# The first turn of a narrow expert: its float32 weight chunk becomes a split one

## The chip, the cores and the metric

The kernel runs on one core of one Trainium2 chip. The metric is the device time of one execution in microseconds (us); lower is better. Three executions of the kernel before took 1529.44, 1529.49 and 1529.63 us, so the median is 1529.49 us.

## What is computed

The reference is a two-layer hybrid encoder on 256 tokens of width 1024. What concerns this change is its last block, a top-2-of-8 expert SwiGLU:

```python
def swiglu(xn, w_gu, w_down):
    g, u = jnp.split(xn @ w_gu, 2, axis=-1)
    return (jax.nn.silu(g) * u) @ w_down

def moe_swiglu(xn, router, w_gu, w_down):
    ...
    for e in range(N_EXPERTS):
        out = out + comb[..., e:e + 1] * swiglu(xn, w_gu[e], w_down[e])
    return out
```

All weights are float32. Each expert has 1024 x 7168 gate and up weights and 3584 x 1024 down weights.

## The kernel before

**Positions, turns, chunks.** The eight experts are processed one after another, in an order that is found at run time; a place in this order is a position (`expert(e, ...)` with e from 0 to 7). Positions 1, 3, 5 and 7 and position 0 are wide (128 token slots); positions 2, 4 and 6 are narrow (64 slots). The hidden width 3584 is worked through in 7 turns (j = 0 to 6) of 512 columns. A turn takes four weight chunks of 128 x 2048 float32 (1 MB each) for gate and up: g0 and g1 for the gate product `pg`, u0 and u1 for the up product `pu`. From the second turn on it also takes two chunks d0 and d1 for the down products of the turn before. Turn 0 has none of these, as nothing is there to multiply yet.

**Split chunks.** `chunk()` takes a landed chunk and splits it in two halves of 1024 columns. For each half ScalarE (ACT) makes a rounded copy hi (line 168, a CAST) and VectorE (DVE) makes the rest lo = raw - hi (line 169, a TENSOR_TENSOR). Tiles for hi and for lo come from rings of NPART = 4 halves each, so that at most two chunks are split ahead of the matmuls that read them. The matmuls (PE) then work on hi and on lo in the faster of the two number formats, `float32r`.

**Narrow positions.** The activations of a narrow position have their hi and lo parts side by side in the 128 columns of the stationary operand, so a split chunk takes four matmuls with hi and four with lo (`narrow`, line 1124). One chunk of each turn, u1, is not split at all: `whole_chunk()` hands out the landed tile, and four float32 matmuls read it directly (line 1193; in the trace each of them is two weight loads and two matmul records). So a narrow turn before has one float32 chunk and three split ones for gate and up, and two split ones for the down products if j is above 0.

**Around turn 0.** The tail of the position before is still under way when the first turn of a narrow position begins: two scalings of its output on DVE (`yl`, line 1235), four scatter products on PE (`so`, lines 1242 and 1243) and four additions to the accumulator on DVE (`accum`, line 1245). Within the turn, `fold` brings the two halves of `pg` together (two copies on ACT, lines 1146 and 1147, one addition on DVE, line 1148), and `gate` makes the hidden values `eh` (an activation on ACT, line 1204, and a product on DVE, line 1206). At the start of the next turn `eh` is transposed on PE (line 1155) and split on ACT and DVE (lines 1054 and 1055).

**Order.** The order of the instructions on each engine is made by a planner from the order of the program, its dependencies and a timing model; `tc.issue_after` adds an edge. `casts` is the list of all hi casts so far: `casts[-1]` is the last one that was written in the program before this point. The DMAs that fetch the chunks are issued by SyncE (SP) in the order of the program, 13 chunks ahead, into a ring of raw tiles; a DMA can start when the last reader of the tile's earlier content is done.

Of the kernel before, what the change touches and what calls it, by code (L numbers as in the profile page):

```python
# [81 lines left out]
def _build(ctx, tc, io, cap):  # L82
# [17 lines left out]
    def f32(ap):  # L100
        return ap.bitcast(F32)
# [4 lines left out]
    def acc_tile(name="acc"):  # L106
        return psA.tile([P, 512], F32, tag="acc", name=name)
# [44 lines left out]
    def split(raw, n=CH, pieces=2, apart=()):  # L152

        cut = (n // 2 + P - 1) // P * P
        parts = []
        for a, b in ((0, cut), (cut, n)):
            if len(parts) in apart:  # L160
                both = rawp.tile([P, CH], F32R, tag="raw", name="apart")
                hi, lo = both[:, :CH // 2], both[:, CH // 2:]
            else:
                hi = hip.tile([P, CH // 2], F32R, tag="hi", name="hi")
                lo = lop.tile([P, CH // 2], F32R, tag="lo", name="lo")
            step = (b - a) * 2 // pieces
            for i in range(0, b - a, step):
                done[:] = (S.copy(hi[:, i:i + step], raw[:, a + i:a + i + step]),  # L168
                           V.tensor_sub(lo[:, i:i + step], raw[:, a + i:a + i + step],  # L169
                                        f32(hi[:, i:i + step])))  # L170
                casts.append(done[0])
            parts.append((hi, lo))

        def at(a, b):
            hi, lo = parts[a >= cut]
            o = cut if a >= cut else 0
            return hi[:, a - o:b - o], lo[:, a - o:b - o]
        return at
# [761 lines left out]
    def fetch():  # L940
        n, (ap, pieces) = next(source)
        ahead.append(load(ap, pieces=pieces, spare=kinds[n] == "s"))
        kinds.append(kinds[-(NRAW + 6)])
# [167 lines left out]
    def whole_chunk():  # L1111
        if not ahead:
            fetch()
        return ahead.popleft()

    def chunk(pieces=2):
        return split(whole_chunk(), pieces=pieces)

    def narrow(ps, xs, ws, first, last):

        n = len(xs)
        for part in range(2):
            for i, (x, w) in enumerate(zip(xs, ws)):
                ins = PE.matmul(ps, x, w[part], start=first and i == part == 0,  # L1124
                                stop=last and part == 1 and i == n - 1)
        return ins

    def expert(e, g, following):
# [4 lines left out]
        def gate_up(j, gu):  # L1133
            pz = acc_tile("gu")
            for kh in range(2):
                w = chunk()
                ws = [w(kk * 512, (kk + 1) * 512) for kk in range(4)]
                moving(pz, [(xg[:, k * P:(k + 1) * P], xg[:, D + k * P:D + (k + 1) * P])
                            for k in range(kh * 4, kh * 4 + 4)],
                       ws, kh == 0, kh == 1)  # L1140
            return pz

        def fold(pg):

            sg = work.tile([P, 512], F32, tag="w2", name="esg", bufs=w2b)
            S.copy(sg[:HALF], pg[HALF:])
            S.copy(sg[HALF:], pg[:HALF])
            V.tensor_add(sg, sg, pg)
            return sg

        def turn_narrow(j, h):

            pt = tr_tile("ht")
            for i in range(4):
                ins = PE.matmul(pt[:, i * HALF:(i + 1) * HALF], h[:, i * P:(i + 1) * P], both,  # L1155
                                start=True, stop=True)
            return pt, ins

        def rows_narrow(j, pt):
            o = (j % 2) * D  # L1160
            side_by_side(ht[:, o:o + 512], pt[:, :4 * HALF])

        def step_narrow(j, h):

            xs = [xg[:, k * P:(k + 1) * P] for k in range(KD)]
            tiles = [(f * 512, (f + 1) * 512) for f in range(4)]  # L1170

            def parts(w):
                return [w(*sl) for sl in tiles]
            pg, pu = acc_tile("gu"), acc_tile("gu")
            g0 = chunk()
            g1 = chunk()
            last = narrow(pg, xs[:4], parts(g0), True, False)
            u0 = chunk()
            if j:
                with tc.issue_after(last.ins):  # L1180
                    pt, last = turn_narrow(j - 1, h)
                with tc.issue_after(casts[-1].ins):
                    rows_narrow(j - 1, pt)
            with tc.issue_after(last.ins):
                narrow(pg, xs[4:], parts(g1), False, True)
            u1 = whole_chunk()
            d0 = chunk() if j else None
            narrow(pu, xs[:4], parts(u0), True, False)
            d1 = chunk() if j else None
            with tc.issue_after(casts[-2 if j else -1].ins):  # L1190
                sg = fold(pg)
            for kk in range(4):
                last = PE.matmul(pu, f32(xs[4 + kk]), u1[:, kk * 512:(kk + 1) * 512],  # L1193
                                 start=False, stop=kk == 3)
            with tc.issue_after(casts[-1].ins):
                h = gate(sg, pu)
            if j:
                down(j - 1, 0, d0)
                down(j - 1, 1, d1)
            return h  # L1200

        def gate(pg, pu):
            sg = pg if two else work.tile([P, 512], F32, tag="w2", name="esg", bufs=w2b)
            S.activation(sg, pg, AF.Silu, scale=g.cw[:, 1:2])
            h = work.tile([P, 512], F32, tag="w2", name="eh", bufs=w2b)
            V.scalar_tensor_tensor(h, pu, g.cw[:, 1:2], sg, op0=ALU.mult, op1=ALU.mult)
            return h
# [11 lines left out]
        def down(j, n, w=None):  # L1219
            if w is None:  # L1220
                w = chunk(4 if e == NE - 1 and j == 6 else 2)
            o = (j % 2) * D
            if two:
                return narrow(py[n], [ht[:, o + f * P:o + (f + 1) * P] for f in range(4)],
                              [w(f * 512, (f + 1) * 512) for f in range(4)], j == 0, j == 6)
            return moving(py[n],
                   [(ht[:, o + f * P:o + (f + 1) * P], ht[:, o + 512 + f * P:o + 512 + (f + 1) * P])
                    for f in range(4)],
                   [w(f * 512, (f + 1) * 512) for f in range(4)], j == 0, j == 6)
# [18 lines left out]
        for j in range(7):  # L1248
            if two:
                h = step_narrow(j, h)  # L1250
                if j == 6:
                    to_rows(6, h)
                if following is not None and j in (3, 5):
                    following.step(j)
                continue
            pg = gate_up(j, 0)
            if j:
                to_rows(j - 1, h)
            pu = gate_up(j, 1)
            h = gate(pg, pu)  # L1260
            if j:
                down(j - 1, 0)
                if j == 6:
                    to_rows(6, h)
                down(j - 1, 1)
            if following is not None and j in (3, 5):
                following.step(j)
# [284 lines left out]
```

## Time and profile before

| what | value |
|---|---|
| median of three runs | 1529.49 us |
| the profiled execution | 1527.87 us, of which the span from the first to the last instruction is 1526.1 us |
| PE busy / weight loads busy | 1499.1 us (98%) / 1298.5 us (85%) |
| DVE busy / ACT busy | 1302.1 us (85%) / 1056.3 us (69%) |
| mean granted TensorE clock | 0.995 |
| expert block | from about 590 us to 1513 us of the span |

Busy time of an engine is the time in which it executes an instruction. A matmul's end is modelled, so PE looks busier than it is; a weight load (PEld) lies beside the matmul before it. DVE, ACT and PE each work through their own queue in order: an instruction that waits holds up all behind it.

### The profile page before, as it was taken

Reading aid. Unit: us, or ns where it says so; the run is one execution under the profiler, and the core shown is the slowest. Engines: PE = TensorE matmul, PEld = TensorE weight load, DVE = VectorE, ACT = ScalarE, POOL = GpSimd, SP = SyncE. Lnnn points to the kernel's source line nnn. Section 1 sums busy time; section 2 is a strip of 40 time slices with the busy share of each in tenths; the row PEclk is TensorE's granted clock in tenths of the full one; section 3 lists DMA queues with packets and bytes.
Section 4 is the critical chain, followed back from the end, with each engine's and each line's share of the span. In section 5 each row is a group of like instructions: output and inputs, shape, how many; then the busy total and the mean of one; then the engine's idle time right before and its main releaser. Section 6 shows DMA issues by size and latency. Waiting matters only on the chain.

```text
span 1526.1 us, 23758 instructions
## 1 busy us (share of the span) xinstructions
PE 1499.1 (98%) x8558; PEld 1298.5 (85%) x8558; DVE 1302.1 (85%) x1735; ACT 1056.3 (69%) x1381; POOL 148.1 (10%) x230
## 2 busy tenths in 40 slices
PE   8999999999999999999999999999999999999996
PEld 8899999999988998888888777888777888777885
DVE  7876677776898867999898999998999998998996
ACT  6554554455576656777777887777887777887775
POOL 4710000001295201000000000000000000000000
PEclk9999999999999999999999999999999999999998
DMA  9754354426644665999999999999999999999940
GB/s 370 278 193 166 138 177 166 140 89 217 228 146 190 214 249 199 372 373 340 356 374 345 383 421 421 391 375 349 380 420 422 404 372 341 394 421 421 388 178 30
DMA packets 65215, 451.44 MB, mean 296 GB/s; under 512 B 7360, under 2 KB 7488, under 8 KB 12480
## 3 DMA queue, kind: packets, MB, share of 16 engines
q1 hardware_dynamic: 65088, 449.83, 76.9%
q8 instruction: 69, 1.13, 0.3%
q14 instruction: 58, 0.48, 0.1%
HBM read 448.75 MB, written 1.05 MB: 295 GB/s over the span
## 4 chain that ended last, share of the span: by engine, by line
PE 88%; POOL 4%; DVE 3%; ACT 2%; issue 1%; DMA 1%; SPq 0%; POOLq 0%; DVEq 0%; ACTq 0%
PE gu L217 8%; PE gu L213 8%; PE gu L212 8%; PE gu L1124 7%; PE acc L206 7%; PE acc L205 7%; PE acc L204 7%; PE py L1124 5%; PE gu L1193 4%; PE py L217 4%; PE py L212 4%; PE py L213 4%; POOL part L780 2%; PE ht L1155 1%; PE gx L1043 1%
## 5 line engine op out<-in xcount | busy, mean ns | idle before, releaser
L169 DVE TENSOR_TENSOR lo<-raw,hi 128x1024 fp32r<-128x1024 f32 (+3 forms) x573 | 673.2, 1209 | 101.1 <-ACT hi L168 81.3
L168 ACT CAST hi<-raw 128x1024 fp32r<-128x1024 f32 (+3 forms) x573 | 569.9, 1031 | 258.4 <-PE acc L205 89.7
L169 DVE TENSOR_TENSOR lo<-spare,hi 128x1024 fp32r<-128x1024 f32 (+1 forms) x226 | 261.7, 1201 | 17.5 <-ACT hi L168 12.1
L168 ACT CAST hi<-spare 128x1024 fp32r<-128x1024 f32 (+1 forms) x226 | 224.0, 1035 | 49.8 <-PE gu L213 27.9
L212 PE MATMUL gu<-hi,xg 128*128 128x512 f32 x560 | 219.5, 392 | 0.0
L213 PE MATMUL gu<-hi,xg 128*128 128x512 f32 x560 | 218.8, 391 | 0.0
L217 PE MATMUL gu<-lo,xg 128*128 128x512 f32 x560 | 157.3, 392 | 0.0
L212 PEld LDWEIGHTS gu<-hi,xg 128*128 128x128 f32 x560 | 105.2, 188 | 22.0 <-ACT hi L168 0.2
L213 PEld LDWEIGHTS gu<-hi,xg 128*128 128x128 f32 x560 | 105.3, 188 | 21.6
L217 PEld LDWEIGHTS gu<-lo,xg 128*128 128x128 f32 x560 | 104.8, 188 | 22.0
L212 PE MATMUL py<-hi,ht 128*128 128x512 f32 x280 | 109.4, 393 | 0.0
L213 PE MATMUL py<-hi,ht 128*128 128x512 f32 x280 | 109.3, 390 | 0.0
L206 PE MATMUL acc<-a2h,lo 128*128 128x256 f32 x336 | 95.4, 284 | 0.0
L205 PE MATMUL acc<-a2l,hi 128*128 128x256 f32 x336 | 95.3, 284 | 0.0
L204 PE MATMUL acc<-a2h,hi 128*128 128x256 f32 x336 | 95.3, 284 | 0.0
L1448 POOL TENSOR_TENSOR fo<-accum,fn 128x512 f32<-128x512 f32 x2 | 2.5, 1272 | 929.5 <-DVE accum L1245 929.5
L217 PE MATMUL py<-lo,ht 128*128 128x512 f32 x280 | 85.0, 396 | 0.0
L1124 PE MATMUL gu<-hi,xg 128*128 128x512 f32 x252 | 72.5, 401 | 0.0
L1124 PE MATMUL gu<-lo,xg 128*128 128x512 f32 x252 | 70.7, 392 | 0.0
L204 PEld LDWEIGHTS acc<-a2h,hi 128*128 128x128 f32 x336 | 64.6, 192 | 0.0
L205 PEld LDWEIGHTS acc<-a2l,hi 128*128 128x128 f32 x336 | 64.6, 192 | 0.0
L206 PEld LDWEIGHTS acc<-a2h,lo 128*128 128x128 f32 x336 | 64.6, 192 | 0.0
(424 smaller groups left out, 3144.1 us busy)
## 6 DMA issues: line engine op xcount, KB each, us to landing
raw<-in_moe_gu SPq DMA_DIRECT2D x139, 1024.0 KB, 7.2
spare<-in_moe_gu SPq DMA_DIRECT2D x85, 1024.0 KB, 7.7
raw<-in_moe_down SPq DMA_DIRECT2D x78, 1024.0 KB, 7.6
spare<-in_moe_down SPq DMA_DIRECT2D x32, 1024.0 KB, 7.5
raw<-in_ffn_gu SPq DMA_DIRECT2D x22, 1024.0 KB, 4.8
raw<-in_pw SPq DMA_DIRECT2D x12, 1024.0 KB, 4.8
raw<-in_ffn_down SPq DMA_DIRECT2D x16, 704.0 KB, 4.1
raw<-in_wk SPq DMA_DIRECT2D x8, 1024.0 KB, 7.2
```

The source lines that it names most:

```text
L168: done[:] = (S.copy(hi[:, i:i + step], raw[:, a + i:a + i + step]), V.tensor_sub(lo[:, i:i + step], raw[:, a + i:a + i + step], f32(hi[:, ...
L169: V.tensor_sub(lo[:, i:i + step], raw[:, a + i:a + i + step], f32(hi[:, i:i + step])))
L204: PE.matmul(ps, a[0], b[0], start=first, stop=False)
L205: PE.matmul(ps, a[0], b[1], start=False, stop=False)
L206: PE.matmul(ps, a[1], b[0], start=False, stop=last)
L212: PE.matmul(ps, a[0], b[0], start=first and i == 0, stop=False)
L213: PE.matmul(ps, a[1], b[0], start=False, stop=False)
L217: ins = PE.matmul(ps, a[0], b[1], start=False, stop=last and i == n - 1)
L780: G.tensor_add(part, part, prod)
L1043: PE.matmul(px[:, kk * P:(kk + 1) * P], xt[:, t * D + d0:t * D + d0 + P], oh[:, t, :], start=t == 0, stop=t == 1)
L1124: ins = PE.matmul(ps, x, w[part], start=first and i == part == 0, stop=last and part == 1 and i == n - 1)
L1193: last = PE.matmul(pu, f32(xs[4 + kk]), u1[:, kk * 512:(kk + 1) * 512], start=False, stop=kk == 3)
```

## The change

In turn 0 of a narrow position, u1 is not taken as a whole chunk any more. It is split like the other chunks and multiplied by `narrow`, with four matmuls on hi and four on lo; the four float32 matmuls of that turn go. Turns 1 to 6 stay as they are. There are three narrow positions, so three chunks of the 336 change. The line of `fold` isn't edited, but in turn 0 `casts[-1]` now is the second cast of u1, where it was the second cast of u0.

```diff
-            u1 = whole_chunk()
+            u1 = whole_chunk() if j else None
             d0 = chunk() if j else None
             narrow(pu, xs[:4], parts(u0), True, False)
+            if j == 0:
+                narrow(pu, xs[4:], parts(chunk()), False, True)
             d1 = chunk() if j else None
             with tc.issue_after(casts[-2 if j else -1].ins):
                 sg = fold(pg)
-            for kk in range(4):
+            for kk in range(4) if j else ():
                 last = PE.matmul(pu, f32(xs[4 + kk]), u1[:, kk * 512:(kk + 1) * 512],
                                  start=False, stop=kk == 3)
```

## Rows read from the trace of the kernel before

**Rows 1.** Page, parts 1 and 4: busy time by engine; engines of the last chain.
```profile
PE 1499.1 (98%) x8558; PEld 1298.5 (85%) x8558; DVE 1302.1 (85%) x1735; ACT 1056.3 (69%) x1381; POOL 148.1 (10%) x230
PE 88%; POOL 4%; DVE 3%; ACT 2%; issue 1%; DMA 1%; SPq 0%; POOLq 0%; DVEq 0%; ACTq 0%
```

**Rows 2.** Windows: three starts of narrow positions (2, 4, 6), then a later turn.
```profile
core 0: us, PE busy (x) PEld busy (x) DVE busy (x) ACT busy (x) POOL busy (x), PEclk, DMA share, GB/s
837.36:854.89 17.53, 17.42 (x73) 12.86 (x72) 17.43 (x20) 13.31 (x17) 0.00 (x0) 1.00 0.93 341
1063.30:1080.49 17.19, 17.19 (x73) 12.87 (x72) 16.93 (x20) 13.91 (x17) 0.00 (x0) 1.00 0.84 308
1288.95:1306.12 17.17, 17.17 (x74) 12.95 (x72) 16.79 (x20) 13.91 (x17) 0.00 (x0) 1.00 0.83 305
1089.80:1103.30 13.50, 13.50 (x59) 9.93 (x57) 13.06 (x14) 11.66 (x15) 0.00 (x0) 1.00 1.01 426
```

**Rows 3.** Chain in order of time (start, length, what): a split and a float32 chunk.
```profile
1087.95 1.81 PE gu L1124 x8
...
1094.36 3.43 PE gu L1193 x8
```

**Rows 4.** Timeline of DVE, position 4, turn 0 (start, length, idle before in brackets).
```profile
1060.83 2.36 DVE L169 TENSOR_TENSOR lo<-raw,hi 128x1024 fp32r<-128x1024 f32 x2 [1.34 <-PE py L217]
...
1069.03 1.23 DVE L169 TENSOR_TENSOR lo<-raw,hi 128x1024 fp32r<-128x1024 f32 x1
1070.16 0.69 DVE L1148 TENSOR_TENSOR esg<-esg,gu 128x512 f32<-128x512 f32 x1
1070.76 1.28 DVE L1245 TENSOR_TENSOR accum<-accum,so 128x512 f32<-128x512 f32 x2
1071.95 2.36 DVE L169 TENSOR_TENSOR lo<-raw,hi 128x1024 fp32r<-128x1024 f32 x2
1074.58 0.75 DVE L1206 SCALAR_TENSOR_TENSOR eh<-gu,cw,esg 128x512 f32<-128x512 f32 x1 [0.26 <-PE gu L1193]
1075.24 4.62 DVE L169 TENSOR_TENSOR lo<-raw,hi 128x1024 fp32r<-128x1024 f32 x4
```

**Rows 5.** Timeline of PE's weight loads, position 4: end of turn 0, end of turn 1's u0.
```profile
1070.30 0.30 PEld L1124 LDWEIGHTS gu<-lo,xg 128*128 128x128 f32 x2 [0.18 <-DVE lo L169]
...
1079.59 0.87 PEld L1124 LDWEIGHTS gu<-lo,xg 128*128 128x128 f32 x4
```

**Rows 6.** Timeline of DVE, position 6, the last splits before turn 1's float32 chunk.
```profile
1299.75 0.75 DVE L1206 SCALAR_TENSOR_TENSOR eh<-gu,cw,esg 128x512 f32<-128x512 f32 x1 [0.38 <-PE gu L1193]
...
1302.15 3.49 DVE L169 TENSOR_TENSOR lo<-raw,hi 128x1024 fp32r<-128x1024 f32 x3
```

**Rows 7.** Timeline of PE's weight loads, position 6, those that read these splits.
```profile
1305.21 0.87 PEld L1124 LDWEIGHTS gu<-lo,xg 128*128 128x128 f32 x4
```

**Rows 8.** Timeline of DVE, position 2, the same place.
```profile
850.56 0.75 DVE L1206 SCALAR_TENSOR_TENSOR eh<-gu,cw,esg 128x512 f32<-128x512 f32 x1
851.22 2.36 DVE L169 TENSOR_TENSOR lo<-raw,hi 128x1024 fp32r<-128x1024 f32 x2
```

**Rows 9.** Timeline of PE's weight loads, position 2, the same place.
```profile
853.06 1.80 PEld L1124 LDWEIGHTS gu<-lo,xg 128*128 128x128 f32 x8
```

**Rows 10.** Timeline of ACT, position 4, turn 0.
```profile
1064.40 1.99 ACT L168 CAST hi<-raw 128x1024 fp32r<-128x1024 f32 x2
1068.76 0.58 ACT L1146 COPY esg<-gu 64x512 f32<-64x512 f32 x1 [2.38 <-PE gu L1124]
```

**Rows 11.** Waits from 780 us on (total us, times, longest): SP's queue, then ACT's casts.
```profile
SPq L147 <- DVE lo L169: 432.4, 178, 14.0
SPq L147 <- PE gu L1193: 77.6, 21, 4.5
...
ACT hi L168 <- PE gu L213: 47.6, 79, 1.2
ACT hi L168 <- PE py L1124: 30.3, 16, 2.2
```

## The prediction

> **What bounds the kernel now.** I read the page first, then the windows, then the timelines of the engines at one place. The page says that PE is busy for 98% of the span and makes up 88% of the chain that ended last [rows 1]. Taken alone, this says that whatever PE is spared comes off the time. But it is a mean over stages, and the change lies in three short ones. The windows cut these out: each goes from the first matmul of a narrow position to the first float32 matmul of its second turn, so it holds turn 0 and three split chunks of turn 1. There PE is busy for 17.42 of 17.53, 17.19 of 17.19 and 17.17 of 17.17 us, and DVE for 17.43, 16.93 and 16.79 us of the same stretches, 98 to 99%; in a later narrow turn it is 13.06 of 13.50 us [rows 2]. So at the starts of narrow positions there are two engines at their limit, not one, and DVE has at most 0.4 us to spare in 17. ACT, at 13.3 to 13.9 us, has over 3 us to spare [rows 2].
>
> Who is ahead of whom is read from the timelines: when DVE ends a lo half, and when PE first loads it. I call the difference the lead. PE makes two weight loads from each lo half; eight loads in a row take 1.80 us and four 0.87, so one follows another after 0.23 us [rows 5, 9]. In position 4 the last lo half of u0 in turn 0 ends at 1069.03 + 1.23 = 1070.26, and PE, which had stood 0.18 us for it, loads it at 1070.30 [rows 4, 5]. In turn 1 the last four lo halves end at 1075.24 + 4.62 = 1079.86; PE begins the loads of u0's lo at 1079.59, and the third of the four, the first that needs the last half, starts some 0.45 us later, at 1080.04: a lead of 0.18 us [rows 4, 5]. In position 6 the same half ends at 1302.15 + 3.49 = 1305.64 and is loaded at 1305.21 + 0.45 = 1305.66, a lead of 0.02 us [rows 6, 7]. In position 2 it ends at 851.22 + 2.36 = 853.58, and the seventh of eight loads from 853.06 starts at 853.06 + 6 x 0.23 = 854.44, a lead of 0.86 us [rows 8, 9]. All three are nearly used up before the change.
>
> **What the change removes.** Per narrow position, four float32 matmuls, eight passes on PE. One such chunk takes 3.43 us of the chain, a split chunk of a narrow position 1.81 us [rows 3]. PE is spared 3.43 - 1.81 = 1.62 us for each, 3 x 1.62 = 4.9 us in all.
>
> **What it adds on DVE.** Two lo halves per position. Two in a row take 2.36 us, four take 4.62 [rows 4]; two more in a busy queue therefore cost 4.62 - 2.36 = 2.26 us. They stand ahead of everything that DVE does for turn 1: PE needs u1's lo to close `pu`, and then six lo halves (g0, g1 and u0 of turn 1) before it comes to the next float32 chunk, the first stretch in which it needs nothing new from DVE. In position 4 DVE has a single gap between the start of its splits (1060.83) and the pacing half (1079.86), 0.26 us ahead of `eh` [rows 4]. In position 6 it is 0.38 us [rows 6]. In position 2 there is none in the place that counts [rows 8]. Those gaps waited for the float32 matmuls, which are gone, so I let them close wholly.
>
> So the pacing half ends later by 2.26 us less the gap, and PE, which could come 1.62 us earlier, waits for it. Against its own old time PE is late by what is left after the lead:
> - position 2: 2.26 - 0.86 = +1.40 us
> - position 4: 2.26 - 0.26 - 0.18 = +1.82 us
> - position 6: 2.26 - 0.38 - 0.02 = +1.86 us
>
> The sum is +5.1 us. PE's saving of 4.9 us doesn't appear in it a second time: it turns into waits for lo (about 1.6 + 1.8 us per position), because it is the later of the two engines that counts. Can DVE start earlier? No: it had stood 1.34 us before g0's first lo half, for the last reader of a buffer of the ring of four [rows 4], and that reader belongs to the position before, which doesn't change.
>
> Does the delay stay? After turn 1's float32 chunk the later turns are as before: PE is busy for 13.50 of 13.50 us in such a turn [rows 2], so it has no gap in which to catch up, and DVE's 0.44 us per turn only rebuild its lead. I carry the whole +5.1 us to the end.
>
> **What it adds on ACT.** Two casts per position, 1.99 us for two [rows 10]. `fold`'s copies now stand behind u1's casts. In position 4 ACT stood idle for 2.38 us before the first copy, since it waited for `pg` [rows 10], and that idle time hides both casts except for the time for which a hi buffer isn't yet free. I take nothing for it and 0 to 0.4 us per position as a bound: 0.4 is what 2.38 leaves beyond 1.99, read as the size of the misfit; it adds 1.2 us at the upper end. If the cover were gone it would cost up to 1.99 us each.
>
> **DMAs.** No DMA is added or moved in order. The raw tile of u1 becomes free when DVE has read it, not when the float32 matmuls have. SP waited 77.6 us for these matmuls in 21 waits, three or so of which now fall under the 178 waits for lo [rows 11]. I cost this at nothing: the longest waits of the casts are for buffers that PE frees [rows 11], and none for a landing stands in the list; the cover are the 13 chunks fetched ahead, about 13 x 1.05 MB / 426 GB/s = 32 us by the rate of a later turn [rows 2]. Without it a late chunk would cost its lateness in full.
>
> **A rule against the trace.** The rows show matmul time at 100% of the stretch, weight loads at 12.9 of 17.2 us, 75%, and DVE at 98% [rows 2]. The Trainium skill (Perfetto Trace Analysis, "Identifying the Most-Contended Engine") says that matmul occupancy is a poor measure of how close PE is to its limit, that the share of weight loads is the better one, and that the engine of the highest occupancy is the one to relieve. By that rule PE has a quarter to spare, DVE alone sets the pace, and the change loads the wrong engine with its whole cost; that is the third rival below. By the leads, both engines are at the limit and part of the cost is covered. The trace agrees with the rule on the direction; on the size the leads decide.
>
> **Rivals.**
> 1. *PE sets the pace after all* (faster). If the planner puts turn 1's splits so that DVE's 2.26 us lie beyond the pacing half, PE keeps its 1.62 us: 1529.5 - 4.9 = 1524.6 us. It decides from a lead of 2.26 + 1.62 = 3.9 us at that half; against it, the leads are 0.86, 0.18 and 0.02. For it, PE is 88% of the chain [rows 1]. Chance 0.07.
> 2. *The additions to the accumulator give way* (no change). Two of them, 1.28 us, lie between u0's last lo and turn 1's splits in position 4 [rows 4]; nothing in this position needs them soon. Planned behind turn 1's u0 they take back 1.2 us per position: 5.1 - 3.6 = +1.5 us, 1531.0 us. Against it, they are ahead in the program and their `so` tiles share a ring with the next transposes. Chance 0.18.
> 3. *DVE alone sets the pace* (slower still). No lead and no gap helps, because the order inside the turns shifts with the new chunk: 3 x 2.26 = +6.8 us, 1536.3 us. Chance 0.13.
>
> **The numbers.** The forecast of +5.1 us has a chance of 0.62. The profiled execution took 1527.87 us, its span and 1.8 us around it, and would take 1533.0; the median of the runs is 1.6 us above it, and from there 1529.49 + 5.1 = 1534.6 us. The range goes up to the third rival with ACT's bound, 1536.3 + 1.2 = 1537.5, and down to 1530.0, which holds the second rival with 1 us to spare; left out are the first and the edges, less than 0.2. About 0.2% (3.1 us) is what a measurement of this kernel can tell from no change. Slower by more: 0.62 + 0.13 = 0.75. Within: 0.18. Faster: 0.07.
>
> **What would show it.** In the profile after: eight float32 passes fewer on PE in each narrow position, six lo halves and six casts more in all; PE idle for some 3 us in turn 0 and turn 1 of each narrow position, its loads released by lo, above all before the lo of turn 1's u0; DVE without a gap from g0's first half to there; the stretch to turn 1's float32 chunk 18.9 to 19.0 us, where it was 17.2 to 17.5; the next turns 13.5 us as before. The prediction is wrong if DVE's queue in those stretches has another order, with the additions behind the splits, or if turn 1's float32 chunk starts at its old distance or earlier.

## The result: twice the forecast loss

The changed kernel takes 1539.24 us in the median of four executions (1537.67 to 1540.38), the kernel before beside it 1529.47. The ratio is 1.0069 with a 95% interval of 1.0056 to 1.0082: slower by 9.8 us, where 5.1 us were forecast. The direction is as forecast, the size is about double, and 1539.24 lies above the range's upper end of 1537.5. In the runs below the kernel before took 1528.24 or 1528.30 us beside them, so each is compared with that and not with 1529.47.

First the page of the changed kernel: busy time by engine, and the rate of the TensorE clock over 40 slices (to be set beside [rows 1]).

```profile
PE 1503.1 (98%) x8558; PEld 1302.4 (85%) x8558; DVE 1308.5 (85%) x1741; ACT 1063.0 (69%) x1387; POOL 148.1 (10%) x230
PEclk9999999999999999999999999999999999999998
```

DVE has six instructions more (the six lo halves) and 6.4 us more to do, ACT six more and 6.7 us. PE is busy for 4.0 us *more*, although in each position eight float32 passes gave way to eight faster ones; a busy PE that gets longer with lighter work is the first hint that something else than the queue of DVE took part. The page's means show nothing of it: the clock stands at 9 in all slices of the expert block.

Where the time lies is read from the same three stretches as [rows 2], from a narrow position's first matmul to turn 1's first float32 matmul. Windows of the changed kernel, positions 2, 4 and 6, with the columns of [rows 2]:

```profile
838.01:861.33 23.32, 19.91 (x74) 14.94 (x72) 21.09 (x23) 17.67 (x21) 0.00 (x0) 0.86 0.90 319
1070.04:1090.01 19.97, 18.11 (x73) 13.49 (x72) 19.57 (x22) 15.43 (x19) 0.00 (x0) 0.91 0.91 333
1298.47:1318.60 20.13, 17.86 (x74) 13.63 (x73) 19.73 (x22) 15.28 (x19) 0.00 (x0) 0.92 0.91 320
```

They are longer by 5.79, 2.78 and 2.96 us, together 11.5 us; the two profiled executions differ by 1540.38 - 1527.87 = 12.5 us. Outside the stretches little is lost and nothing won back: the first starts 0.65 us later than before; from its end to the start of the second it is 208.41 us before and 208.71 after, from the end of the second to the start of the third 208.46 us in both kernels, and from the end of the third to the end of the program 219.98 us before and 220.10 after. PE, full in [rows 2], now waits in each stretch (3.4, 1.9 and 2.3 us not busy). And the granted clock in them is 0.86, 0.91 and 0.92, where it was 1.00.

The next view shows what PE waits for. Timeline of its weight loads in the changed kernel, position 4 (start, length, what; in brackets the idle time before and what ended it):

```profile
1080.53 0.30 PEld L1124 LDWEIGHTS gu<-lo,xg 128*128 128x128 f32 x2 [0.87 <-DVE lo L169]
1082.26 0.30 PEld L1124 LDWEIGHTS gu<-lo,xg 128*128 128x128 f32 x2 [1.44 <-DVE lo L169]
1083.40 0.50 PEld L1124 LDWEIGHTS gu<-lo,xg 128*128 128x128 f32 x2 [0.84 <-DVE lo L169]
1084.00 1.61 PEld L1124 LDWEIGHTS gu<-hi,xg 128*128 128x128 f32 x4
1086.33 1.14 PEld L1155 LDWEIGHTS ht<-kept,eh 128*128 128x128 f32 x8 [0.72 <-DVE eh L1208]
1087.39 0.77 PEld L1124 LDWEIGHTS gu<-hi,xg 128*128 128x128 f32 x4
1088.20 1.77 PEld L1124 LDWEIGHTS gu<-lo,xg 128*128 128x128 f32 x8
1090.01 0.19 PEld L1195 LDWEIGHTS gu<-raw,xg 128*128 128x128 f32 x1
```

The waits for lo are the ones that were forecast. Two things were not. The last wait is for `eh`, and behind it four hi and eight lo loads run through without a stop. And the four hi loads at 1084.00 take 1.61 us, where four take 0.77 at 1087.39. DVE's timeline of the same place tells the first of them:

```profile
1077.52 1.22 DVE L169 TENSOR_TENSOR lo<-spare,hi 128x1024 fp32r<-128x1024 f32 x1
...
1079.26 1.22 DVE L169 TENSOR_TENSOR lo<-spare,hi 128x1024 fp32r<-128x1024 f32 x1
...
1080.99 4.63 DVE L169 TENSOR_TENSOR lo<-raw,hi 128x1024 fp32r<-128x1024 f32 x4
1085.53 0.75 DVE L1208 SCALAR_TENSOR_TENSOR eh<-gu,cw,esg 128x512 f32<-128x512 f32 x1
1086.19 2.36 DVE L169 TENSOR_TENSOR lo<-raw,hi 128x1024 fp32r<-128x1024 f32 x2
```

The two added halves are those at 1077.52 and 1079.26. Then four halves of turn 1 come ahead of `eh`; in [rows 4] it was two, and four after it. DVE is as late as forecast: the pacing half, the last of u0 in turn 1, ends at 1086.19 + 2.36 = 1088.55, 18.51 us after the start of the stretch, and could let PE reach the float32 chunk after 19.0. But PE comes to that half about 1 us later than it is ready, because the transposes of `eh` stand in its queue ahead of these twelve loads. In position 6 it is the same: four halves of turn 1 ahead of `eh`, where it was two.

In position 2 the order differed from the other two positions before the change already. DVE's timelines there, first of the kernel before (it goes on in [rows 8]), then of the changed kernel:

```profile
844.23 3.49 DVE L169 TENSOR_TENSOR lo<-raw,hi 128x1024 fp32r<-128x1024 f32 x3
...
848.83 1.23 DVE L169 TENSOR_TENSOR lo<-raw,hi 128x1024 fp32r<-128x1024 f32 x1
```

```profile
844.88 3.49 DVE L169 TENSOR_TENSOR lo<-raw,hi 128x1024 fp32r<-128x1024 f32 x3
...
849.48 1.22 DVE L169 TENSOR_TENSOR lo<-raw,hi 128x1024 fp32r<-128x1024 f32 x1
...
851.21 3.50 DVE L169 TENSOR_TENSOR lo<-raw,hi 128x1024 fp32r<-128x1024 f32 x3
854.62 0.75 DVE L1208 SCALAR_TENSOR_TENSOR eh<-gu,cw,esg 128x512 f32<-128x512 f32 x1
855.28 2.36 DVE L169 TENSOR_TENSOR lo<-raw,hi 128x1024 fp32r<-128x1024 f32 x2
```

Before, `eh` stood behind four halves of turn 1. In the changed kernel the first two halves at 844.88 are those of u1, so five halves of turn 1 stand ahead of `eh`, and the pacing half is the first of the two at 855.28. It ends at 855.28 + 1.22 = 856.50, 18.49 us after the start.

The second is the clock. Timeline of the weight loads in position 2, and windows over the places with slow loads in positions 2, 4 and 6:

```profile
854.76 0.50 PEld L1124 LDWEIGHTS gu<-lo,xg 128*128 128x128 f32 x2 [2.57 <-DVE lo L169]
855.42 1.98 PEld L1155 LDWEIGHTS ht<-kept,eh 128*128 128x128 f32 x8 [0.16 <-DVE eh L1208]
857.27 1.40 PEld L1124 LDWEIGHTS gu<-hi,xg 128*128 128x128 f32 x4
858.77 2.46 PEld L1124 LDWEIGHTS gu<-lo,xg 128*128 128x128 f32 x6
861.33 0.48 PEld L1195 LDWEIGHTS gu<-raw,xg 128*128 128x128 f32 x2
```

```profile
855.42:861.33 5.91, 5.91 (x20) 4.98 (x18) 3.68 (x4) 3.99 (x6) 0.00 (x0) 0.50 0.87 333
1084.00:1086.33 2.33, 2.33 (x6) 1.32 (x4) 2.33 (x4) 0.48 (x1) 0.00 (x0) 0.50 1.02 380
1312.20:1314.75 2.55, 2.40 (x7) 1.33 (x5) 2.55 (x4) 0.70 (x1) 0.00 (x0) 0.50 0.80 225
```

The granted clock is 0.50 in each: TensorE runs at 1.2 GHz in place of 2.4. In position 2 PE is busy without a break from the transposes to the float32 chunk, at half the rate. Before, the transposes, four hi and eight lo loads took 854.89 - 851.36 = 3.53 us there; two of the lo loads now stand ahead of the transposes, and without these two, 0.23 us each, the same work took 3.07 us. Now it takes 5.91. In positions 4 and 6 the slow time lies mostly in the wait for `eh`.

### The profile page after: what moved, and what is told of

Read it like the earlier page. It is cut to its first block, busy times and chain, and to the rows that moved or that the text cites. A ratio compares the mean times of both kernels' runs of the same rounds, so it can differ in the third digit from the quotient of the medians.

```text
span 1538.7 us, 23771 instructions
## 1 busy us (share of the span) xinstructions
PE 1503.1 (98%) x8558; PEld 1302.4 (85%) x8558; DVE 1308.5 (85%) x1741; ACT 1063.0 (69%) x1387; POOL 148.1 (10%) x230
## 3 DMA queue, kind: packets, MB, share of 16 engines
q8 instruction: 69, 1.13, 0.3%
## 5 line engine op out<-in xcount | busy, mean ns | idle before, releaser
L169 DVE TENSOR_TENSOR lo<-raw,hi 128x1024 fp32r<-128x1024 f32 (+2 forms) x577 | 677.7, 1210 | 108.6 <-ACT hi L168 92.5
L168 ACT CAST hi<-raw 128x1024 fp32r<-128x1024 f32 (+2 forms) x577 | 574.0, 1030 | 260.9 <-PE acc L205 90.4
L212 PE MATMUL gu<-hi,xg 128*128 128x512 f32 x560 | 219.4, 392 | 0.0
L213 PE MATMUL gu<-hi,xg 128*128 128x512 f32 x560 | 218.7, 391 | 0.0
L217 PE MATMUL gu<-lo,xg 128*128 128x512 f32 x560 | 157.0, 392 | 0.0
L217 PEld LDWEIGHTS gu<-lo,xg 128*128 128x128 f32 x560 | 104.8, 188 | 22.0
L1124 PE MATMUL gu<-lo,xg 128*128 128x512 f32 x264 | 77.8, 406 | 6.6 <-DVE lo L169 6.6
L1124 PE MATMUL gu<-hi,xg 128*128 128x512 f32 x264 | 78.4, 411 | 0.8 <-ACT hi L168 0.8
L1124 PEld LDWEIGHTS gu<-lo,xg 128*128 128x128 f32 x264 | 49.9, 193 | 20.7 <-DVE lo L169 10.6
```

The lines of the kernel that those rows point to most:

```text
L212: PE.matmul(ps, a[0], b[0], start=first and i == 0, stop=False)
L213: PE.matmul(ps, a[1], b[0], start=False, stop=False)
L217: ins = PE.matmul(ps, a[0], b[1], start=False, stop=last and i == n - 1)
```

## The experiments

The theory after the result: DVE's two added halves set the pace of these stretches, as forecast (A); `eh` behind four or five halves of turn 1 adds to it (A1); and the waits let the clock fall, which adds again (A2). The rivals: the loss has nothing to do with DVE's load in these turns (B), or the order and the clock are marks of the waits and cost nothing.

### Room on DVE: the additions to the accumulator left out

```diff
-                V.tensor_add(a, a, pz)
+                if e + 1 not in NARROW:
+                    V.tensor_add(a, a, pz)
```

In the kernel before:

> The kernel before, without the additions to the accumulator (VectorE, 4 per position, 0.6 us each in a busy queue) at the end of positions 1, 3 and 5, that is in the first turns of the narrow positions; the output lacks these experts' parts. Control for the next run. If TensorE sets the pace of these turns in the kernel before (its windows there are full), the 2.4 us of VectorE per position are not on the path: 1529.5 us, within 1.5 us. If VectorE already set the pace: 1529.5 - 3 x 2.4 = 1522 us.

In the changed kernel:

> The changed kernel with the same 12 additions left out. Theory A (the two added lo halves on VectorE at the start of a narrow position make TensorE wait): the four additions, 2.4 us, make room for the 2.3 us that were added, so the loss goes and TensorE keeps some or all of its 1.6 us per position: 1524.6 to 1529.5 us, at or below its control, with the granted clock at 1.00 in the three stretches. Rival B (the loss comes from another order elsewhere, not from VectorE's load in these turns): about 10 us above its control as with the additions, 1539 us.

Measured: 1528.02 us for the kernel before without the additions (ratio to the kernel before 1.0000, interval 0.9990 to 1.0009) and 1528.60 for the changed kernel without them (1.0001, 0.9992 to 1.0011). The stretches of positions 2 and 4, first of the control, then of the changed kernel (position 6 is as position 4, with 17.18 and 16.48 us):

```profile
836.89:854.07 17.18, 17.18 (x74) 12.93 (x73) 15.29 (x16) 13.71 (x17) 0.00 (x0) 1.00 0.95 349
1062.46:1079.65 17.19, 17.19 (x74) 12.93 (x73) 14.55 (x16) 13.81 (x17) 0.00 (x0) 1.00 0.81 291
```

```profile
838.72:856.87 18.15, 16.62 (x74) 12.60 (x72) 17.97 (x19) 15.65 (x19) 0.00 (x0) 1.00 0.96 357
1065.28:1081.76 16.48, 16.32 (x74) 12.61 (x72) 16.48 (x18) 16.07 (x20) 0.00 (x0) 1.00 0.95 349
```

The control says that in the kernel before PE sets the pace by a hair: with DVE down to 14.6 to 15.3 us its stretches are 17.2 us, 0.35 us shorter in position 2 and no shorter in the others. The changed kernel says that the loss needs DVE to be full: with 2.4 us less on DVE it is gone to within 1.5 us, the width of the interval to either side, and the clock stays at 1.00. Rival B falls. The run does not separate DVE's load from the order of its queue, for in positions 4 and 6 the planner put `eh` back behind two halves of turn 1; the next runs do.

Of the 1.62 us that PE is spared, only 0.7 show in positions 4 and 6, where DVE is full at 16.48 of 16.48 us: even with that room DVE sets the pace there. Position 2 is 1.0 us longer than its control, and there `eh` still stands behind five halves. One line of DVE and one of PE's weight loads in position 2:

```profile
853.60 2.34 DVE L169 TENSOR_TENSOR lo<-raw,hi 128x1024 fp32r<-128x1024 f32 x2
853.79 0.97 PEld L1155 LDWEIGHTS ht<-kept,eh 128*128 128x128 f32 x8 [0.43 <-issue]
```

The pacing half, the first of the two, is ready at 854.8, 16.1 us after the start, but the transposes start only at 853.79 (`eh` is done at 852.94 + 0.74 = 853.68), and the work behind them takes until 856.87, 3.08 us at full clock. So the late `eh` alone, with no fall of the clock, makes this stretch 18.15 - 16.48 = 1.7 us longer than the two others.

### The order of `eh`

```diff
             g0 = chunk()
-            g1 = chunk()
+            with tc.issue_after(hidden[0].ins) if j == 1 else nullcontext():
+                g1 = chunk()
...
-            V.scalar_tensor_tensor(h, pu, g.cw[:, 1:2], sg, op0=ALU.mult, op1=ALU.mult)
+            hidden[:] = [V.scalar_tensor_tensor(h, pu, g.cw[:, 1:2], sg, op0=ALU.mult, op1=ALU.mult)]
```

> The changed kernel, where the second chunk of turn 1 (g1) of a narrow position may be split only after eh, the hidden values of turn 0, are made, as stood in the queue of VectorE before. In the profile after, eh came behind four lo halves of turn 1 and the transposes behind eh, in TensorE's queue, stood ahead of 3.7 us of matmuls whose splits were long ready. Theory A1 (this order is part of the excess of the loss over the 5.1 us forecast): the way to turn 1's float32 chunk gets shorter by about 1.0 us in positions 4 and 6 and by 1 to 3 us in position 2, 1534 to 1536.5 us. If the order of eh does not matter: 1539 us.

Measured: 1534.87 us (1534.71 to 1534.95), ratio 1.0044 (1.0027 to 1.0061): about 6.6 us above the kernel before (1528.24 beside it). Its stretches:

```profile
838.56:857.43 18.87, 17.16 (x74) 12.44 (x73) 18.87 (x22) 16.22 (x19) 0.00 (x0) 1.00 0.90 304
1065.82:1085.87 20.05, 18.05 (x74) 13.83 (x73) 20.05 (x23) 16.91 (x20) 0.00 (x0) 0.91 0.87 312
1294.29:1313.16 18.87, 16.43 (x74) 12.68 (x72) 18.87 (x22) 16.15 (x20) 0.00 (x0) 1.00 0.87 307
```

Here `eh` stands behind two halves of turn 1 in all three positions. Positions 2 and 6 are the forecast's case pure: DVE is busy for all of 18.87 us, the clock stays at 1.00, and 18.9 to 19.0 us were forecast. So A1 holds: the order of `eh`, with what the clock does behind it, was worth 20.13 - 18.87 = 1.3 us in position 6 and 23.32 - 18.87 = 4.5 us in position 2. In position 4 the clock still fell (mean 0.91), and the stretch is 1.2 us longer than the two others. PE had waited 2.04 and 0.84 us for lo ahead of it there. In position 6 it had waited 1.54 and 1.44 us, and the clock stayed; in the changed kernel the same two waits, at the same distance from the start of the stretch, stand in position 6, and there it fell. PE's weight loads in position 6, first with `eh` ahead, then of the changed kernel:

```profile
1305.89 0.30 PEld L1124 LDWEIGHTS gu<-lo,xg 128*128 128x128 f32 x2 [1.54 <-DVE lo L169]
1307.62 0.30 PEld L1124 LDWEIGHTS gu<-lo,xg 128*128 128x128 f32 x2 [1.44 <-DVE lo L169]
```

```profile
1310.08 0.30 PEld L1124 LDWEIGHTS gu<-lo,xg 128*128 128x128 f32 x2 [1.54 <-DVE lo L169]
1311.81 0.36 PEld L1124 LDWEIGHTS gu<-lo,xg 128*128 128x128 f32 x2 [1.44 <-DVE lo L169]
```

What decides stays open.

### The clock held up by matmuls with zeros

```diff
+    zero = ident[:HALF, HALF:]
...
+                for _ in range(fills[i // 2] if part and i % 2 == 0 else 0):
+                    PE.matmul(ps[:HALF], zero, f32(w[0][:HALF]), start=False, stop=False)
                 ins = PE.matmul(ps, x, w[part], start=first and i == part == 0,
...
+            last = narrow(pg, xs[:4], parts(g0), True, False, (2, 1) if j == 1 else (0, 0))
...
+                narrow(pu, xs[4:], parts(chunk()), False, True, (0, 1))
```

> The changed kernel with four further float32 matmuls with zero weights (0.86 us each) in TensorE's queue at the places where it waits for lo in turns 0 and 1 of each narrow position: they add zeros to the sums. Theory A2 (the waits let the clock fall to half, which costs time of its own in position 2, where 5.9 us of work that takes 3.5 us at full clock ran at half): the granted clock stays at 1.00 in the three stretches and position 2 gets back about 2.4 us, positions 4 and 6 almost nothing: 1536 to 1537.5 us. If the clock's fall is only a mark of the waits and costs nothing: 1539 us; if the fillers lie on the path: up to 3 x 3.4 us more.

Measured: 1537.28 us (1536.71 to 1538.66), ratio 1.0063 (1.0046 to 1.0079). That is 9.0 us above the kernel before, against 9.8 without the fillers; the intervals overlap, so the times alone do not tell the two kernels apart. The stretches of the profiled execution:

```profile
837.12:857.47 20.35, 20.34 (x82) 13.43 (x80) 19.70 (x22) 15.36 (x19) 0.00 (x0) 1.00 0.92 318
1065.90:1086.28 20.38, 20.36 (x81) 13.35 (x80) 19.72 (x22) 15.37 (x19) 0.00 (x0) 1.00 0.91 326
1294.68:1315.04 20.36, 20.34 (x81) 13.43 (x80) 19.62 (x22) 15.23 (x18) 0.00 (x0) 1.00 0.89 310
```

More matmuls, and a shorter stretch: position 2 goes from 23.32 to 20.35 us, with the clock at 1.00 throughout. The planner also put `eh` behind four halves of turn 1 there, where it had been five. But by the run without the additions the whole late order costs 1.7 us there, and the gain is 2.97 us in spite of the fillers; so some 1.3 us of it at least are the clock's. Its whole size is read from the slow work itself, 5.91 us in place of 3.07. Positions 4 and 6 become 0.4 and 0.2 us longer: PE is full with fillers.

Both remedies together:

> The changed kernel with both remedies: eh ahead of g1, and the float32 matmuls with zero weights in TensorE's waits. If the excess of the loss over the forecast is the order of eh and the fall of the clock, and nothing else, position 4, the one stretch with a fallen clock in the run with eh ahead (20.05 us), comes to 18.9 us as the others, 1.2 us less in all, unless the fillers (3.4 us in each stretch, in waits of some 4 us) lie on the path themselves: 1533.5 to 1535.5 us.

Measured: 1537.21 us (ratio 1.0060, 1.0045 to 1.0076), above what was expected. All three stretches are 20.07 us long, with PE busy for 20.07 of them at a clock of 1.00: the fillers lie on the path themselves. This run says nothing on the rest of position 4's excess.

### Half the dose

The kernel with `eh` ahead of g1, where only the first half of u1 is split in turn 0:

```diff
-                narrow(pu, xs[4:], parts(chunk()), False, True)
+                u1 = whole_chunk()
...
+                V.tensor_sub(lo, u1[:, :CH // 2], f32(hi))
+                narrow(pu, xs[4:6], [(hi[:, i:i + 512], lo[:, i:i + 512]) for i in (0, 512)],
+                       False, False)
...
-            for kk in range(4) if j else ():
+            for kk in range(4) if j else (2, 3):
```

> The kernel of the run with eh ahead of g1, but only the first half of u1 is split in turn 0; its second half stays float32 (two float32 matmuls). Half the dose: one lo half more on VectorE (1.13 us), 0.81 us less on TensorE. Theory A (VectorE's queue sets when the stretch from a narrow position's first matmul to turn 1's float32 chunk ends): these stretches, 17.2 to 17.5 us before and 18.9 us with the whole chunk split and the clock at 1.00, come to 17.7 to 18.0 us, the whole to about 1.7 us above the kernel before, 1530 us, with no fall of the clock. Rival (any split of u1 breaks the order, whatever its size): as with the whole chunk, 6 us above.

Measured: 1530.10 us (1529.42 to 1531.60) beside 1528.30, ratio 1.0014 (1.0005 to 1.0023). The stretches:

```profile
837.73:855.75 18.02, 17.22 (x73) 12.62 (x72) 17.82 (x21) 15.42 (x19) 0.00 (x0) 1.00 0.86 299
1064.15:1081.90 17.75, 17.35 (x74) 12.53 (x72) 17.75 (x21) 15.40 (x19) 0.00 (x0) 1.00 0.85 293
1290.31:1308.05 17.74, 17.11 (x73) 12.68 (x72) 17.74 (x21) 15.46 (x19) 0.00 (x0) 1.00 0.83 290
```

One lo half less shortens positions 2 (to 18.02) and 6 (to 17.74) by 0.9 and 1.1 us against 18.87; the price of a half in the queue was put at 1.13. DVE is full again in positions 4 and 6, PE isn't; in position 2 DVE waits 0.20 us for `esg`, the input of `eh` that ACT makes. `eh` stands behind two halves of turn 1 in all three, as in the run with `eh` ahead. So the loss follows the number of lo halves on DVE, at a full clock and with one order, and the whole is 1.8 us above the kernel before, where 1.7 were expected.

### The lo halves of u1 on GpSimd

Both halves on GpSimd, in the kernel with `eh` ahead of g1:

```diff
-                           V.tensor_sub(lo[:, i:i + step], raw[:, a + i:a + i + step],
+                           (sub or V.tensor_sub)(lo[:, i:i + step], raw[:, a + i:a + i + step],
...
-                narrow(pu, xs[4:], parts(chunk()), False, True)
+                narrow(pu, xs[4:], parts(split(whole_chunk(), sub=G.tensor_sub)), False, True)
```

> The kernel with eh ahead of g1, with both lo halves of u1 in turn 0 made by GpSimd, which stands idle there, in place of VectorE. Theory A: VectorE's queue is as long as before and TensorE has 1.6 us less per position; if a lo half takes GpSimd about 2.5 us (twice its 1.27 us for 512 columns in the trace) and VectorE is not slowed, the stretches are 16.5 to 17.2 us, 1525 to 1528 us in all. If GpSimd slows VectorE while both run, or takes 4 us and more for a half so that TensorE waits for u1's lo, the gain is lost: 1530 to 1535 us. Rival B (VectorE's load does not matter): 1534.9 us as with VectorE.

And the second half of u1 and the second half of turn 1's g1, further apart:

```diff
+                           (G if len(parts) in pool else V).tensor_sub(
...
+                g1 = chunk(pool=(1,) if j == 1 else ())
...
+                narrow(pu, xs[4:], parts(chunk(pool=(1,))), False, True)
```

> As the run before, but GpSimd makes the second lo half of u1 in turn 0 and the second lo half of g1 in turn 1, so that its two halves lie some 4 us apart and are needed later. VectorE's load is the same. If GpSimd's length of a half is what TensorE waits for, this is faster than the run before by up to 2 us; if VectorE is slowed by GpSimd, the same as the run before.

Measured: 1534.32 us (ratio 1.0042, 1.0028 to 1.0056) and 1540.68 us (1.0078, 1.0063 to 1.0094). The first is 6.0 us above the kernel before, not told apart from the 6.6 with both halves on DVE; the second is 12.4 us above. Neither regains the loss. Timelines of GpSimd and then of DVE in position 4 of the first:

```profile
1070.81 5.74 POOL L169 TENSOR_TENSOR lo<-spare,hi 128x1024 fp32r<-128x1024 f32 x2 [222.76 <-PE gu L1124]
```

```profile
1071.79 2.50 DVE L169 TENSOR_TENSOR lo<-raw,hi 128x1024 fp32r<-128x1024 f32 x1
1074.22 1.27 DVE L1248 TENSOR_TENSOR accum<-accum,so 128x512 f32<-128x512 f32 x2
```

and of both in position 4 of the second, GpSimd first:

```profile
1074.45 2.39 POOL L169 TENSOR_TENSOR lo<-spare,hi 128x1024 fp32r<-128x1024 f32 x1 [221.93 <-PE gu L1125]
```

```profile
1074.52 3.40 DVE L169 TENSOR_TENSOR lo<-raw,hi 128x1024 fp32r<-128x1024 f32 x1
```

A lo half takes GpSimd 2.4 to 3.1 us, and a lo half of DVE that runs beside it takes 2.50 and even 3.40 us in place of 1.22; in the second case the excess of 2.2 us is nearly all of GpSimd's 2.39. There GpSimd ends at 1076.84 and DVE's half at 1077.92, 1.1 us later, about the length of an undisturbed half: as if it had done nothing until GpSimd was through. DVE's additions, which read from PSUM, keep their 0.64 us each beside GpSimd. So moving a half to GpSimd gives DVE's time away again. In the first run the three stretches are 20.01, 18.62 and 18.91 us long, DVE is busy for 57.3 us of them in all, and it was 57.8 with both halves of u1 on DVE. The Trainium skill (GPSIMD Engine Reference, "1. Specifications") says that GpSimd's way to SBUF is shared with VectorE, with contention for instructions that read two tensors there; the trace agrees, and adds the price. Theory A is neither helped nor hurt by these two: they took hardly any load off DVE.

## Why the prediction was right in direction and wrong in size

**That DVE's load decides, and that the change is slower: right.** The loss is gone when DVE has 2.4 us less to do, and with one order it follows the number of halves. The view that carried it was the windows with DVE at 98 to 99% and the leads of 0.02 to 0.86 us.

**The term of 2.26 us per two halves, the leads and the gaps: right.** In the changed kernel the pacing half ends 18.49, 18.51 and 18.49 us after the start of the stretch in positions 2, 4 and 6. That is 2.27, 1.95 and 1.80 us later than before, and 2.26 less the gap, 2.26, 2.00 and 1.88 us, was forecast. Where nothing else intervened, in positions 2 and 6 with `eh` ahead, PE reached the float32 chunk 0.39 us behind that half, after 18.87 us: +1.34 and +1.70 us against a forecast of +1.40 and +1.86.

**That the delay stays: right.** 208.46 us between the second and the third stretch and 220 us behind them, as before.

**That ACT and the DMAs cost nothing: right, as far as it shows.** With `eh` ahead PE waits 0.78 and 0.84 us for hi in position 2, and still the stretch is 18.87 us long. No idle time of ACT or DVE in the three stretches of the changed kernel ended with the landing of a chunk.

**That PE's saving of 4.9 us turns into waits: right, and stronger than told.** Even without the additions most of it isn't to be had.

**The pacing half: wrong.** This step of the sum failed. It took the last lo half of turn 1's u0 for what PE waits on last, on the unspoken ground that the order of DVE's queue stays. The planner put `eh` behind four halves of turn 1 in place of two in positions 4 and 6 and behind five in place of four in position 2, and PE's queue holds the transposes of `eh` ahead of the last ten or twelve loads. The last wait is then for `eh`: the transposes start 16.3 us into the stretch in positions 4 and 6 and 17.4 in position 2, and what stands behind them takes 3.53 us at full clock, 3.07 in position 2. That alone gives 19.8 and 20.5 us in place of 18.9: 0.9 us each for the order in positions 4 and 6, and 1.6 in position 2. The prediction named another order of that queue as what would make it wrong, but only in the direction of a gain. Why the planner chose this order is not shown.

**The clock: not in the sum at all.** The prediction let PE wait some 3 us per position and costed what PE does afterwards at its old rate; it put this term at nothing without a reason. In position 2 the 3.07 us behind the waits took 5.91 at half the clock: 2.8 us. In positions 4 and 6 the work of 3.53 us took 1090.01 - 1086.33 = 3.68 and 1318.60 - 1314.75 = 3.85 us, 0.15 and 0.3 more, since most of the slow time was spent waiting.

For the profiled execution this makes the bill:

| position | DVE's queue | order of `eh` | clock | measured |
|---|---|---|---|---|
| 2 | 1.34 | 1.61 | 2.84 | 5.79 |
| 4 | 1.71 | 0.92 | 0.15 | 2.78 |
| 6 | 1.70 | 0.94 | 0.32 | 2.96 |
| all | 4.75 | 3.47 | 3.31 | 11.53 |

DVE's part is what the run with `eh` ahead measured in positions 2 and 6. In position 4 the clock fell again in that run, so its part is an estimate: the end of the pacing half, 18.51, and the same 0.39 us. The split between the order and the clock is read from the timelines of the changed kernel; the 1.6 us has its counterpart in the 1.7 us of the run without the additions. By the medians the excess over the forecast is 4.7 us, less than the 6.8 us of order and clock in the profiled execution, which was the slowest of the four. These spread over 2.7 us, and their mean granted clock goes with them: 0.994 at 1537.67, 0.993 at 1538.73, 0.991 at 1539.76 and 0.990 at 1540.38 us; the kernel with `eh` ahead spreads over 0.24 us. How much of the median the clock takes was not measured.

**The third rival** (DVE alone, 1536.3 us) put the size nearer, but by luck: it let no lead and no gap count, and the leads and gaps did cover their part, as positions 2 and 6 with `eh` ahead show. The Trainium skill's rule on the most contended engine (Perfetto Trace Analysis, "Identifying the Most-Contended Engine") put the direction right. That VectorE alone sets the pace, as the prediction read it, is not borne out: relieved of 2.4 us per position in the kernel before, it left the time where it was (ratio 1.0000).

No version tried that computes the whole beats the kernel before. Its float32 chunk, slow on PE, is what keeps DVE's queue short enough.

## What to carry to other kernels

Where two engines are full in the same stretch, work moved from one to the other is a loss of what it adds on the second less its lead, and the lead is read from the timelines, half by half. When a planner sets the order, ask also which instruction the in-order queue behind the new work holds back (here `eh`), and price the new order, not only the new length. And where TensorE will have to wait, cost the work behind the wait at both clock levels.

## What the runs showed of the hardware

- In the three stretches of the changed kernel TensorE's clock fell to half, and the longest wait ahead of a fall was 2.57 us. In position 4 waits of 0.87, 1.44 and 0.84 us with some matmuls between them preceded the fall. In position 6, two waits of 1.54 and 1.44 us preceded one in the changed kernel and none in the kernel with `eh` ahead.
- A VectorE subtraction of 128x1024 float32 from SBUF took 3.40 us in place of 1.22 beside one GpSimd subtraction of the same size, which took 2.39 us; an addition that reads PSUM was not slowed.
- A float32 chunk costs PE 3.43 us, a chunk split into two parts 1.81 us [rows 3], and yet the float32 one was the cheaper of the two here, where the splitting engine was full.
